# Experts ranked on the chip: 64 places for four of them, some float32 down products, and weights laid out in 4 KB rows

## The chip, the cores and the metric

One Trainium2 chip; the program runs on one of its cores. The metric is the device time of one execution in microseconds, the median over runs: lower is better.

## What is computed

A decoder trunk of two layers on 256 tokens of width 1024. Each layer has a mixing part (dilated attention beside a gated delta rule) and a channel part. The channel part of layer 1 is a choice of experts, and the change is there:

```python
logits = (x @ router_w).astype(jnp.float32)
top_val, top_idx = lax.top_k(logits, TOP_K)            # TOP_K = 2 of N_EXPERTS = 8
top_w = jax.nn.softmax(top_val, axis=-1)
gates = jnp.sum(jax.nn.one_hot(top_idx, N_EXPERTS) * top_w[..., None], axis=-2)
for e in range(N_EXPERTS):
    y = y + gates[..., e:e + 1] * swiglu(x, w_gate[e], w_up[e], w_down[e])
```

with `swiglu(x, g, u, d) = (silu(x @ g) * (x @ u)) @ d`, `g` and `u` of 1024 x 3584 and `d` of 3584 x 1024, all float32. One expert's weights are 44 MB, those of the eight 352 MB.

## The kernel before

Products need about float32 accuracy. A weight is therefore split into two float32r parts, `whi` (a cast on ACT, L100 and L102) and `wlo` (the rest, a subtraction on DVE, with GpSimd taking half of every third piece, L105). Activations are split the same way, and a row block of 128 weights costs **three products** (L414 to L416): high by high, high by low, low by high.

`Stream` (L50) holds all weights in the order of their use, in *pieces* of two row blocks by 512 columns, 512 KB. `dma_to` (L72) issues a piece's load on SP, straight from the weight matrix, in rows of 2 KB; every third piece of the experts comes as two halves in the smaller buffers (`rawh`). `advance` (L86) splits pieces ahead of their use. `caps(raw, split)` bounds the pieces loaded ahead and those split ahead; the experts have (21, 5), and (18, 5) while layer 1's output projection runs. Buffers are 36 of 4 KB and 16 of 2 KB a partition.

The experts (`moe`, L1399): `route` (L1199) finds the two experts of each token and the token's place in their lists; meanwhile `dense` (L1378) computes the first 512 hidden columns of expert 0 for all tokens. Each expert has 128 places. `gather` (L1274) takes the tokens of a pair of experts by products with one-hot rows (`Pt`). Then the experts come in order 0 to 7, each in seven chunks `c` of 512 hidden columns: `expert` (L1372) makes gate (`mg`) and up (`mu`) products, 8 row blocks each; `hidden` (L1311) makes silu(gate) times up, `hidden_t` transposes and splits it; `down` (L1359) multiplies the chunk before by its 4 row blocks of down weights for both halves `f` of the output (`oe`). `scatter` (L1342) adds an expert's result to its tokens' rows. A chunk is so 12 pieces, 24 row blocks, 72 products. Work of the helpers is put between the products by `tick`; the framework's scheduler then sets the order on each engine.

`overflow` (L1441) is a loop over all experts behind a branch, for lists longer than 128 tokens. Then comes the last normalization, and the result is written.

```python
self.CAP_MOE0 = (18, 5)
self.CAP_MOE = (21, 5)
```

Of the kernel before, what the change touches and what calls it, by code (L numbers as in the profile page):

```python
# [18 lines left out]
P = 128  # L19
# [8 lines left out]
D_EXP = 3584  # L28
NEG = -1.0e30
# [14 lines left out]

class Stream:
    """Weights in the order of their use, in pieces of two row blocks: DRAM to SBUF, then their float32 values
    split exactly into two float32r parts. caps() bounds the pieces loaded ahead and those split ahead."""

    def __init__(self, k, raw, spl):
        self.k, self.raw_cap, self.spl_cap = k, raw, spl  # L50
        self.subs = []
        self.key = {}
        self.raw = {}
        self.split = {}
        self.n_dma = 0
        self.n_split = 0
        self.retired = 0
        self.done_subs = set()
        self.share = False
        self.moe = 0  # L60
        self.SHARE, self.HALVES = 3, 3
# [4 lines left out]
    def add(self, key, src, kb, n):  # L66
        first = len(self.subs)
        for h in range(0, kb, 2):
            self.subs.append((src[:, h:h + 2], n))
        self.key[key] = list(range(first, len(self.subs)))  # L70

    def dma_to(self, i):  # L72
        while self.n_dma <= min(i, len(self.subs) - 1):
            src, n = self.subs[self.n_dma]
            q = self.k.nc.sync
            if self.n_dma >= self.moe and self.n_dma % self.HALVES == 0:
                t = [self.k.k2([P, 512], name="rawh") for _ in range(2)]
                for k in range(2):
                    q.dma_start(t[k][:, :n], src[:, k])
            else:  # L80
                t = self.k.k4([P, 2, 512], name="raw")
                q.dma_start(t[:, :, :n], src)
# [3 lines left out]
    def advance(self, need=0):  # L86
        k, nc = self.k, self.k.nc
        top = min(max(self.retired + self.spl_cap - 1, need), len(self.subs) - 1)
        while self.n_split <= top:
            i = self.n_split  # L90
            n = self.subs[i][1]
# [5 lines left out]
            if isinstance(raw, list):  # L97
                parts = [(raw[j][:, None], j, j + 1) for j in range(2)]
                for r, a, b in parts:
                    k.last_act = nc.scalar.copy(hi[:, a:b, :n], r[:, :, :n])  # L100
            else:
                k.last_act = nc.scalar.copy(hi[:, :, :n], raw[:, :, :n])  # L102
                parts = [(raw[:, j:j + 1], j, j + 1) for j in range(2)] if share else [(raw, 0, 2)]
            for r, a, b in parts:
# [21 lines left out]
class Kern:  # L126
# [7 lines left out]
    # ---------------------------------------------------------------- interleaving  # L134
# [46 lines left out]
    # ---------------------------------------------------------------- small helpers  # L181
# [36 lines left out]
    # ---------------------------------------------------------------- constants  # L218
# [47 lines left out]
        # rows of an odd block of 16 and columns of the block before it  # L266
# [18 lines left out]
    def rope_tables(self):  # L285
        """cos and sin of position * frequency, with the angle reduced exactly by multiples of 2 pi."""
# [25 lines left out]
        # [c | c] and [-s | s]  # L312
# [33 lines left out]
    # ---------------------------------------------------------------- weight plan  # L346
    def plan(self):
        W, A = self.W, self.A

        def sq(w, r0, kb, c0, n):  # L350
            return w[r0 * P:(r0 + kb) * P, c0:c0 + n].rearrange("(k p) n -> p k n", p=P)

        for l in range(DEPTH):
            wi = A["w_in"][l]
            for kg in range(2):
                W.add(("at", l, 0, 0, kg), sq(wi, 4 * kg, 4, 0, 512), 4, 512)
            for half in range(2):
                for part in range(3):
                    for kg in range(2):
                        W.add(("qb", l, half, part, kg), sq(wi, 4 * kg, 4, C_QB + part * 1024 + half * 512, 512), 4, 512)  # L360
            for g in range(3):
                for part in range(1 if g == 0 else 0, 3):
                    for kg in range(2):
                        W.add(("at", l, g, part, kg), sq(wi, 4 * kg, 4, part * 1536 + g * 512, 512), 4, 512)
                for nm, c0 in ((("z", C_Z),), (), (("ga", C_GA), ("gb", C_GB)))[g]:
                    for f in range(2):
                        for kg in range(2):
                            W.add((nm, l, f, kg), sq(wi, 4 * kg, 4, c0 + f * 512, 512), 4, 512)
            for f in range(2):
                W.add(("ba", l, f, 0), sq(A["w_branch_a"][l], 0, 4, f * 512, 512), 4, 512)  # L370
                for kg in range(2):
                    W.add(("bb", l, f, kg), sq(A["w_branch_b"][l], 4 * kg, 4, f * 512, 512), 4, 512)
            for kg in range(2):
# [1214 lines left out]
```

## Time and profile before

| | |
|---|---|
| median of three runs | 2021.1 us (2020.6 to 2021.52) |
| the profiled execution: its span | 2023.3 us; nothing further is recorded around it |
| busy in the span | PE 97%, PE's weight loads 81%, DVE 81%, ACT 63%, GpSimd 30% |
| moved | 513.65 MB, 254 GB/s mean; 278544 packets |
| weight loads' queue (SP) | 276144 packets, 504.11 MB, 70.6% of the 16 DMA engines |

Busy shares are means over stages that have different limits; slices and stretches tell them apart. Matmuls overlap in the pipeline, so PE's pace is read from the starts of neighbours and not from the duration of one (some 0.39 us). A wait is put down to the instruction that came last.

### The profile page before, as it was taken

The page shows a single profiled execution, that of the slowest core. Times are in us where ns is not written, and L with a number is a line of the kernel's source. Part 1 is how long each engine was busy: PE and PEld are TensorE (multiplying, and loading weights), DVE is VectorE, ACT ScalarE, POOL GpSimd, SP SyncE. Part 2 cuts the span into 40 slices and gives each one's busy share as a digit, 9 for nine tenths or more (in the row PEclk, how much of TensorE's full clock was granted, in tenths as well). Part 3 has the DMA queues.
Part 4 walks back from the last instruction along what each step waited for, and adds up shares of the span by engine and source line. Part 5 has one row for each costly group of instructions (what it writes and reads, how often), then busy time and mean ns, then how long its engine had stood idle before and what let it go on. Part 6 is the DMA issues. An engine that isn't in the chain of part 4 may idle for free. (4 is left out here: it accounts for less than half of the span.)

```text
span 2023.3 us, 30086 instructions
## 1 busy us (share of the span) xinstructions
PE 1960.1 (97%) x10143; PEld 1640.3 (81%) x10143; DVE 1644.2 (81%) x2208; ACT 1270.8 (63%) x1958; POOL 613.9 (30%) x484
## 2 busy tenths in 40 slices
PE   8889999999999999999999999999999999999995
PEld 7878888888888878888788788887888878888784
DVE  7886757665566976666789989999899998999997
ACT  5554546444444555554388778777787777877784
POOL 4341211000003422210334334343343433434342
PEclk9899999999999999999999999999999999999998
DMA  8344344664664353537589999999999999999991
GB/s 297 105 157 150 132 132 154 197 222 131 236 215 127 118 177 95 181 127 239 205 292 373 354 350 347 363 366 350 350 357 359 366 355 334 371 358 370 351 351 42
DMA packets 278544, 513.65 MB, mean 254 GB/s; under 512 B 29904, under 2 KB 32176, under 8 KB 278384
## 3 DMA queue, kind: packets, MB, share of 16 engines
q1 hardware_dynamic: 276144, 504.11, 70.6%
q0 software_dynamic: 2240, 7.56, 1.1%
q8 instruction: 81, 1.33, 0.3%
q14 instruction: 79, 0.65, 0.1%
HBM read 506.09 MB, written 5.51 MB: 253 GB/s over the span
## 5 line engine op out<-in xcount | busy, mean ns | idle before, releaser
L105 DVE TENSOR_TENSOR wlo<-raw,whi 128x1024 fp32r<-128x1024 f32 (+1 forms) x726 | 921.7, 1291 | 121.4 <-ACT whi L102 118.5
L102 ACT CAST whi<-raw 128x1024 fp32r<-128x1024 f32 (+1 forms) x726 | 744.8, 1046 | 78.0 <-DVE wlo L105 18.9
L105 POOL TENSOR_TENSOR wlo<-rawh,whi 128x512 fp32r<-128x512 f32 x224 | 390.7, 1744 | 593.4 <-ACT whi L100 415.3
L105 DVE TENSOR_TENSOR wlo<-rawh,whi 128x512 fp32r<-128x512 f32 x224 | 269.1, 1201 | 6.3 <-ACT whi L100 6.3
L100 ACT CAST whi<-rawh 128x512 fp32r<-128x512 f32 x448 | 256.1, 622 | 18.8 <-PE mg L415 9.8
L415 PE MATMUL oe<-wlo,hte 128*128 128x512 f32 x448 | 180.7, 403 | 0.4
L415 PE MATMUL mu<-wlo,xe 128*128 128x512 f32 x440 | 172.6, 392 | 6.6 <-DVE wlo L105 6.3
L414 PE MATMUL oe<-whi,hte 128*128 128x512 f32 x448 | 175.7, 392 | 0.0
L416 PE MATMUL oe<-whi,hte 128*128 128x512 f32 x448 | 175.2, 391 | 0.0
L414 PE MATMUL mu<-whi,xe 128*128 128x512 f32 x440 | 171.6, 390 | 0.0
L416 PE MATMUL mu<-whi,xe 128*128 128x512 f32 x440 | 171.5, 390 | 0.0
L414 PE MATMUL mg<-whi,xe 128*128 128x512 f32 x440 | 171.4, 390 | 0.0
L416 PE MATMUL mg<-whi,xe 128*128 128x512 f32 x440 | 171.4, 390 | 0.0
L415 PE MATMUL mg<-wlo,xe 128*128 128x512 f32 x440 | 171.3, 389 | 0.0
L105 POOL TENSOR_TENSOR wlo<-raw,whi 128x512 fp32r<-128x512 f32 x53 | 84.3, 1603 | 102.5 <-ACT whi L102 84.0
L566 PE MATMUL qb<-xhl,whi 128*128 128x256 f32 x384 | 113.4, 296 | 0.0
L569 PE MATMUL qb<-xhl,whi 128*128 128x256 f32 x384 | 110.9, 289 | 0.0
L571 PE MATMUL qb<-xhl,wlo 128*128 128x256 f32 x384 | 110.8, 289 | 0.0
L414 PE MATMUL at<-whi,xhl 128*128 128x512 f32 x256 | 108.1, 422 | 0.0
L415 PE MATMUL at<-wlo,xhl 128*128 128x512 f32 x256 | 102.6, 401 | 3.3 <-DVE wlo L105 3.3
L415 PEld LDWEIGHTS mu<-wlo,xe 128*128 128x128 f32 x440 | 82.6, 188 | 28.4 <-DVE wlo L105 10.9
L416 PE MATMUL at<-whi,xhl 128*128 128x512 f32 x256 | 101.9, 398 | 0.0
(421 smaller groups left out, 3875.7 us busy)
## 6 DMA issues: line engine op xcount, KB each, us to landing
raw<-in_w_in SPq DMA_DIRECT2D x168, 512.0 KB
raw<-in_moe_w_gate SPq DMA_DIRECT2D x168, 512.0 KB
raw<-in_moe_w_up SPq DMA_DIRECT2D x167, 512.0 KB
raw<-in_moe_w_down SPq DMA_DIRECT2D x113, 512.0 KB
rawh<-in_moe_w_down SPq DMA_DIRECT2D x222, 256.0 KB
rawh<-in_moe_w_up SPq DMA_DIRECT2D x114, 256.0 KB
rawh<-in_moe_w_gate SPq DMA_DIRECT2D x112, 256.0 KB
raw<-in_ffn_w_down SPq DMA_DIRECT2D x22, 512.0 KB
```

The lines of the kernel that those rows point to most:

```text
L100: k.last_act = nc.scalar.copy(hi[:, a:b, :n], r[:, :, :n])
L102: k.last_act = nc.scalar.copy(hi[:, :, :n], raw[:, :, :n])
L105: ins = (nc.gpsimd if share and a else nc.vector).tensor_tensor(lo[:, a:b, :n], r[:, :, :n], f32(hi)[:, a:b, :n], op=OP.subtract)
L414: nc.tensor.matmul(o, lhsT=xh, rhs=hi[:, kk, :n], start=st, stop=False)
L415: nc.tensor.matmul(o, lhsT=xh, rhs=lo[:, kk, :n], start=False, stop=False)
L416: nc.tensor.matmul(o, lhsT=xl, rhs=hi[:, kk, :n], start=False, stop=en)
L566: nc.tensor.matmul(o, lhsT=hi[:, kk, w], rhs=self.xhl[k // 2][:, k % 2, :S], start=(k == 0 and b % 2 == 0), stop=False, skip_group_check=True)
L569: nc.tensor.matmul(o, lhsT=hi[:, kk, w], rhs=self.xhl[k // 2][:, k % 2, S:], start=False, stop=False, skip_group_check=True)
L571: nc.tensor.matmul(o, lhsT=lo[:, kk, w], rhs=self.xhl[k // 2][:, k % 2, :S], start=False, stop=(k == 7), skip_group_check=True)
```

## The change

Weights are put in another order before the launch: every piece is one run in memory, 128 rows of 4 KB (`trunk` for everything but the experts, `moe` for those, indexed by expert and piece). `rawh` and GpSimd's part in the experts' splits go; the limits of pieces loaded ahead become 12 and 14.

On the chip `route` counts each expert's tokens and ranks the experts. Expert 0 keeps rank 0, because its first columns are under way; ranks 1 to 7 go to the others by rising count. Ranks 1 to 4 are *narrow*: 64 places. Their 64 columns of high parts and 64 of low parts of the activations stand side by side as one 128-column operand, so a row block takes **two products** (`packed`); rows 64 to 127 of the result are then folded onto rows 0 to 63 (a copy on ACT and an addition on DVE, for gate and for up). The other ranks stay at 128 places. The order of ranks is 0, 1, 5, 2, 6, 3, 7, 4: wide and narrow in turn. Which weights are loaded is known on the chip only: SP reads the expert's number into a register and adds it to the address.

Down products come one expert later, with the same chunk of the next expert; those of the last one come at the end, half by half. In wide experts the down products of chunks 0, 2, 4 and 6 use the weights and activations unsplit, as **one float32 product** (`unsplit`). The loop for overflow runs if any list is longer than its places.

```diff
+RANKS = (0, 1, 5, 2, 6, 3, 7, 4)
+NARROW = (1, 2, 3, 4)
+def moe_pieces(nm, c, j):
+    first = 12 * c + {"mg": 0, "mu": 4, "md": 8}[nm] + 2 * j
+    return first, first + 1
 class Stream:
     def dma_to(self, i):
         while self.n_dma <= min(i, len(self.subs) - 1):
-            src, n = self.subs[self.n_dma]
-            q = self.k.nc.sync
-            if self.n_dma >= self.moe and self.n_dma % self.HALVES == 0:
-                t = [self.k.k2([P, 512], name="rawh") for _ in range(2)]
-                for k in range(2):
-                    q.dma_start(t[k][:, :n], src[:, k])
-            else:
-                t = self.k.k4([P, 2, 512], name="raw")
-                q.dma_start(t[:, :, :n], src)
+            src, n, _ = self.subs[self.n_dma]
+            if callable(src):
+                src = src()
+            t = self.k.k4([P, 2, 512], name="raw")
+            self.k.nc.sync.dma_start(t[:, :, :n], src[:, :2 * n].rearrange("p (k n) -> p k n", k=2))
...
     def advance(self, need=0):
...
+            if plain:
+                self.split[i] = (raw, None, 2, n)
+                self.n_split += 1
+                self.dma_to(self.n_split + self.raw_cap - 1)
+                continue
...
-            share = self.share or (i >= self.moe and i % self.SHARE == 0)
+            share = self.share
...
     def plan(self):
...
+            def src():
+                if r not in self.reg:
+                    self.reg[r] = self.nc.values_load(self.eidi[0:1, r:r + 1], engines=(mybir.EngineType.SP,), min_val=0,
+                                                      max_val=NE - 1)
+                return A["moe"][bass.ds(self.reg[r], 1), j].rearrange("o p n -> (o p) n")
...
+        for i, r in enumerate(RANKS):
+            for c in range(7):
+                for nm in ("mg", "mu"):
+                    for kg in range(2):
+                        add(nm, r, c, kg)
+                if i:
+                    for f in range(2):
+                        add("md", RANKS[i - 1], c, f)
+        for f in range(2):
+            for c in range(7):
+                add("md", RANKS[-1], c, f)
+    def plain(self, r, c):
+        return r not in NARROW and c in self.PLAIN
...
     def route(self):
...
+        cnt = self.small([P, 3, 8], "cnt")
+        nc.vector.tensor_copy(cnt[:, 0], ps[:, 0:8])
+        nc.vector.scalar_tensor_tensor(cnt[:, 1], cnt[:, 0], 8.0, io8, op0=OP.mult, op1=OP.add)
+        nc.vector.memset(cnt[:, 1, 0:1], -1.0)
...
+        nc.vector.tensor_tensor(m8[:, 0], col(cnt[:, 1]), row(cnt[:, 1]), op=OP.is_lt)
+        nc.vector.tensor_reduce(cnt[:, 2], m8[:, 0], axis=AX.X, op=OP.add)
...
     def hidden(self, res, key):
...
+        def folded(a, dst):
+            if not nar:
+                return a
+            nc.scalar.copy(dst[:64], a[64:])
+            nc.vector.tensor_tensor(dst[:64], dst[:64], a[:64], op=OP.add)
+            return dst[:64]
...
+    def packed(self, keys, o, x, first=True, last=True):
...
+                nc.tensor.matmul(o, lhsT=x(k0 + kk), rhs=hi[:, kk], start=first and i == 0 and kk == 0, stop=False)
+                nc.tensor.matmul(o, lhsT=x(k0 + kk), rhs=lo[:, kk], start=False, stop=last and end)
...
+    def unsplit(self, keys, o, x, first=True, last=True):
...
+                nc.tensor.matmul(o, lhsT=x(k0 + kk), rhs=w[:, kk], start=first and i == 0 and kk == 0, stop=last and end)
...
     def moe(self):
...
+                if i:
+                    self.run(self.down(RANKS[i - 1], c))
+        for f in range(2):
+            for c in range(7):
+                self.run(self.down(RANKS[-1], c, (f,)))
...
     def overflow(self):
...
-        with tc.If(n > P):
+        with tc.If(n > 0):
...
     def build(self):
...
-        self.CAP_MOE0 = (18, 5)
-        self.CAP_MOE = (21, 5)
+        self.CAP_MOE0 = (12, 5)
+        self.CAP_MOE = (14, 5)
+        self.PLAIN = (0, 2, 4, 6)
```

The order on PE, before, where an expert's down products end and the gate products of the next chunk begin (`hte` is the transposed hidden part, `xe` the gathered tokens):

```order
L414 MATMUL oe<-whi,hte 128x512
L415 MATMUL oe<-wlo,hte 128x512
L416 MATMUL oe<-whi,hte 128x512
L414 MATMUL mg<-whi,xe 128x512
L415 MATMUL mg<-wlo,xe 128x512
L416 MATMUL mg<-whi,xe 128x512
L414 MATMUL mg<-whi,xe 128x512
```

Now, in the first narrow expert (`xen`; lines are those of the changed kernel). `htp` is the unsplit hidden part, `raw` the weights as they were loaded:

```order
L1495 MATMUL mg<-wlo,xen 128x512
L1494 MATMUL mg<-whi,xen 128x512
L1439 MATMUL ht<-ident,mgs 128x128 x4
L1508 MATMUL oe<-raw,htp 128x512
L1495 MATMUL mg<-wlo,xen 128x512
L1494 MATMUL mg<-whi,xen 128x512
L1495 MATMUL mg<-wlo,xen 128x512
L1494 MATMUL mg<-whi,xen 128x512
```

Three products a row block have become two, and the down products, with one float32 product each, stand between gate products. The weights of this first `oe` are the ninth piece of the chunk, while those of the gate products around it are the first and second.

The order on DVE, before, at the end of a chunk:

```order
L105 TENSOR_TENSOR wlo<-rawh,whi 128x512
L105 TENSOR_TENSOR wlo<-raw,whi 128x1024
L1322 TENSOR_TENSOR mgs<-mgs,mu 128x512
L105 TENSOR_TENSOR wlo<-raw,whi 128x1024
L105 TENSOR_TENSOR wlo<-rawh,whi 128x512
L105 TENSOR_TENSOR wlo<-raw,whi 128x1024 x2
L1339 TENSOR_TENSOR hte<-ht,hte 128x4x128
```

Now, for one chunk of a narrow expert whose down part is float32:

```order
L162 TENSOR_TENSOR wlo<-raw,whi 128x1024 x7
L1414 TENSOR_TENSOR mgs<-mgs,mg 64x512
L162 TENSOR_TENSOR wlo<-raw,whi 128x1024 x2
L1414 TENSOR_TENSOR mus<-mus,mu 64x512
L1425 TENSOR_TENSOR mgs<-mgs,mus 64x512
L1447 TENSOR_TENSOR htn<-ht,htn 128x4x64
L162 TENSOR_TENSOR wlo<-raw,whi 128x1024 x5
```

The halves `rawh` are gone, so every split is 1024 columns on DVE; the folds (L1414) and the narrower second part (`htn`) have come in.

The order on SP now, where the last of the experts' numbers are read (`eidi`; the loads ahead are those of expert 0, whose address is fixed; `cnti` tells whether the overflow loop runs):

```order
L418 TENSOR_LOAD eidi
L418 ISA x2
L418 TENSOR_LOAD eidi
L418 ISA x2
L140 DMA raw<-in_moe 128x1024 x2
L1591 TENSOR_LOAD cnti
L1591 ISA x2
L140 DMA raw<-in_moe 128x1024 x2
L140 ISA
L140 DMA raw<-in_moe 128x1024
L140 ISA
```

Before, SP had loads alone here, with fixed addresses. Now it reads seven numbers between the 33rd and the 53rd piece of the experts, and behind the loads of rank 0 each load has a register operation (`ISA`) of its own.

## Rows read from the trace of the kernel before

**Rows 1.** The page's second part: busy tenths of PE, DVE and the DMA engines, and GB/s, in 40 slices of 50.6 us.

```profile
PE   8889999999999999999999999999999999999995
DVE  7886757665566976666789989999899998999997
...
DMA  8344344664664353537589999999999999999991
GB/s 297 105 157 150 132 132 154 197 222 131 236 215 127 118 177 95 181 127 239 205 292 373 354 350 347 363 366 350 350 357 359 366 355 334 371 358 370 351 351 42
```

**Rows 2.** Busy time of each engine by stretches of the second half: stretch, length, then busy us (instructions) of PE, PEld (weight load), DVE, ACT and POOL, granted clock, DMA share, GB/s.

```profile
993.00:1030.00 37.00, 36.51 (x204) 29.94 (x203) 28.49 (x66) 21.03 (x36) 10.14 (x8) 1.00 0.48 164
...
1196.00:1316.00 120.00, 119.66 (x554) 98.42 (x553) 113.27 (x106) 94.37 (x132) 46.66 (x28) 1.00 0.96 346
...
1556.00:1676.00 120.00, 118.50 (x537) 97.19 (x536) 114.23 (x102) 91.65 (x126) 48.43 (x28) 1.00 1.00 366
1676.00:1796.00 120.00, 119.66 (x553) 98.42 (x552) 113.14 (x105) 93.94 (x133) 46.70 (x27) 1.00 0.96 345
```

**Rows 3.** Waits between 1200 and 1900 us: engine, line, what it waited for: us in total, times, longest.

```profile
PEld mu L415 <- DVE wlo L105: 7.2, 8, 1.8
...
PE mu L415 <- DVE wlo L105: 3.5, 5, 1.4
```

**Rows 4.** The same stretch, waits of SP's DMA queue (L79 and L82 issue the weight loads).

```profile
SPq L79 <- DVE wlo L105: 203.9, 110, 5.7
SPq L79 <- PE oe L415: 54.9, 30, 1.9
```

**Rows 5.** PE's instructions in order of time, the first and the last of 42 products: start us, duration us, engine, line, out<-in.

```profile
1502.28 0.39 PE L414 MATMUL mg<-whi,xe 128*128 128x512 f32 x1
...
1511.57 0.39 PE L416 MATMUL mu<-whi,xe 128*128 128x512 f32 x1
```

**Rows 6.** PE's instructions on the tile `mg` over the whole run: count, durations in ns, first and last start.

```profile
L414 PE MATMUL mg<-whi,xe x440: 387/389/479, 1024.0 to 1982.1; 128*128 128x512 f32 x147
```

**Rows 7.** PE in order of time, the last product of the experts.

```profile
2002.11 0.40 PE L416 MATMUL oe<-whi,hte 128*128 128x512 f32 x1
```

**Rows 8.** The page's fifth part: one of the three products of a row block, for each kind of weights (count | busy us, mean ns | idle before).

```profile
L415 PE MATMUL oe<-wlo,hte 128*128 128x512 f32 x448 | 180.7, 403 | 0.4
L415 PE MATMUL mu<-wlo,xe 128*128 128x512 f32 x440 | 172.6, 392 | 6.6 <-DVE wlo L105 6.3
...
L415 PE MATMUL mg<-wlo,xe 128*128 128x512 f32 x440 | 171.3, 389 | 0.0
```

**Rows 9.** PE in order of time at the float32 products of `kkq` (x8 is eight records, two for a product); `qb` are split products of 256 columns.

```profile
98.36 0.28 PE L569 MATMUL qb<-xhl,whi 128*128 128x256 f32 x1
98.48 0.28 PE L571 MATMUL qb<-xhl,wlo 128*128 128x256 f32 x1
98.61 1.89 PE L728 MATMUL kkq<-kq 128*128 128x256 f32 x8
100.15 0.47 PE L566 MATMUL qb<-xhl,whi 128*128 128x256 f32 x1
100.45 0.28 PE L569 MATMUL qb<-xhl,whi 128*128 128x256 f32 x1
```

**Rows 10.** Groups of instructions between 1200 and 1900 us: line, engine, operation, out<-in, shape, count | busy us, mean ns | idle time before and what ended it.

```profile
L105 DVE TENSOR_TENSOR wlo<-raw,whi 128x1024 fp32r<-128x1024 f32 x315 | 423.7, 1369 | 13.2 <-ACT whi L102 13.0
L102 ACT CAST whi<-raw 128x1024 fp32r<-128x1024 f32 x316 | 327.5, 1051 | 23.2 <-PE mg L415 10.0 <-PE oe L416 5.9 <-issue 2.8
L105 POOL TENSOR_TENSOR wlo<-rawh,whi 128x512 fp32r<-128x512 f32 x159 | 276.7, 1740 | 426.4 <-ACT whi L100 299.4 <-DVE wlo L105 36.7 <-DMA raw<-in_moe_w_gate 24.5
...
L1322 DVE TENSOR_TENSOR mgs<-mgs,mu 128x512 f32<-128x512 f32 x39 | 26.7, 684 | 10.3 <-ACT whi L100 7.5 <-issue 1.6 <-PE mu L416 1.2
...
L1356 DVE TENSOR_TENSOR x<-x,sc 128x512 f32<-128x512 f32 x24 | 15.4, 685 | 7.0 <-PE sc L1354 7.0
...
L1349 DVE SCALAR_TENSOR_TENSOR ol<-oe,gs,oh 128x512 fp32r<-128x512 f32 x12 | 8.9, 744 | 0.1
...
L1307 DVE COPY gs<-PT 128x1 f32<-128x1 f32 x6 | 0.9, 152 | 0.9 <-ACT PT L1306 0.9
```

**Rows 11.** DVE in order of time in a stretch of the trunk where GpSimd shares no split.

```profile
405.94 2.36 DVE L105 TENSOR_TENSOR wlo<-raw,whi 128x1024 fp32r<-128x1024 f32 x2
408.21 0.75 DVE L213 TENSOR_TENSOR xhl<-tp,xhl 128x256 fp32r<-128x256 f32 x2
```

**Rows 12.** A number read from SBUF into SP's registers and the register operation behind it (L1444): durations min/median/max in ns.

```profile
L1444 SPq TENSOR_LOAD <-cnti x1: 463/463/463, 1021.8 to 1021.8; - x1
L1444 SPq FUSED_REGOPS  x1: 181/181/181, 1022.3 to 1022.3; - x1
```

**Rows 13.** Issues of loads into the tile `raw`: durations min/median/max in ns, first and last start.

```profile
L82 SPq DMA_DIRECT2D raw<-in_moe_w_gate x168: 367/406/1343, 959.3 to 1946.1; - x168
```

**Rows 14.** Stretches as in rows 2: one in which only the copies of zeros of L282 move, and two in the experts.

```profile
42.00:44.00 2.00, 2.00 (x19) 2.00 (x18) 2.00 (x7) 1.79 (x3) 1.20 (x1) 1.00 0.91 369
1240.00:1242.00 2.00, 2.00 (x11) 1.65 (x10) 2.00 (x3) 1.74 (x3) 1.08 (x1) 1.00 1.06 409
1260.00:1280.00 20.00, 20.00 (x91) 16.48 (x90) 19.11 (x19) 16.16 (x23) 7.64 (x6) 1.00 1.03 390
```

More of the change, by code (lines that the diff above doesn't have):

```diff
@@ new lines, in plan, with piece @@
+        first = 0
+        for key, _, _, _, kb, _, n in trunk_blocks():
+            W.add(key, [A["trunk"][first + j] for j in range(kb // 2)], n)
+            first += kb // 2
+        self.reg = {}
+        def piece(r, j):
+            if r == 0:
+                return A["moe"][0, j]
+            def src():
[3 more added lines that the diff above has]
+                return A["moe"][bass.ds(self.reg[r], 1), j].rearrange("o p n -> (o p) n")
+            return src
@@ new lines, in route @@
+        eid = self.small([P, 8], "eid")
+        by_rank(eid, io8)
+        self.eidi = self.small([P, 8], "eidi", 1, I32)
+        nc.vector.tensor_copy(self.eidi, eid)
+        yield
+        self.rk0, self.gt0 = rk, gt
+        self.rk = self.small([P, 2, 8], "rkr")
+        self.gt = self.small([P, 2, 8], "gtr")
+        for t in range(2):
+            by_rank(self.rk[:, t], rk[:, t])
+            by_rank(self.gt[:, t], gt[:, t])
+        yield
+        cap = self.small([P, 8], "cap")
+        nc.vector.memset(cap, float(P))
@@ L1262, in route, with place @@
+        self.cnti = self.small([P, 1], "cnti", 1, I32)
+        nc.vector.tensor_copy(self.cnti, cnt[:, 1, 0:1])
         for t in range(2):
             nc.scalar.mul(self.x[t], self.x[t], ALPHA)
[L1265 removed]
+    def place(self, i):
         nc = self.nc
[L1268 to L1269 removed]
+        self.Pt[i] = Pt = self.k2([P, 2, 2, P], F32R, name="Pt")
+        for r in RANKS[max(2 * i - 1, 0):2 * i + 1]:
             for t in range(2):
[L1271 to L1272 removed]
@@ L1357, in scatter, with down @@
             yield
-    def down(self, e, c):
+    def down(self, r, c, fs=(0, 1)):
         if c == 0:
-            self.oe = [self.bg("oe"), self.bg("oe")]
-        self.finish([("ht", e, c)])
-        ht = self.ht.pop((e, c))
-        def xf(k, t):
-            return ht[:, k - 4 * c, :P], ht[:, k - 4 * c, P:]
-        for f in range(2):
-            yield from self.gemm([(("md", e, c, f), 4 * c)], {0: self.oe[f]}, xf, first=(c == 0), last=(c == 6), tiles=(0,))
-            if c == 6:
-                self.add_chain(self.scatter(e, f, self.oe[f]), ("scat", e, f), 1)
@@ L1372, in expert @@
-    def expert(self, e, c, nm):
-        a = self.acc(nm)
-        xf = hlf(self.xe[e // 2])
-        yield from self.gemm([((nm, e, c, kg), 4 * kg) for kg in range(2)], {e % 2: a}, xf, tiles=(e % 2,))
+            if fs[0] == 0:
+                self.oe = {}
+            for f in fs:
+                self.oe[f] = self.bg("oe")
+        self.finish([("ht", r, c)])
+        ht = self.ht[r, c]
+        for f in fs:
+            keys, ends = [(("md", r, c, f), 0)], dict(first=(c == 0), last=(c == 6))
+            if r in NARROW:
+                yield from self.packed(keys, self.oe[f], lambda k: ht[:, k], **ends)
+            elif self.plain(r, c):
+                yield from self.unsplit(keys, self.oe[f], lambda k: ht[:, k], **ends)
+            else:
+                yield from self.gemm(keys, {0: self.oe[f]}, lambda k, t: (ht[:, k, :P], ht[:, k, P:]), tiles=(0,), **ends)
+            if c == 6:
+                self.add_chain(self.scatter(r, f, self.oe[f]), ("scat", r, f), 1)
@@ L1376, in expert @@
+    def expert(self, r, c, nm):
+        a = self.acc(nm)
+        keys = [((nm, r, c, kg), 4 * kg) for kg in range(2)]
+        x = self.xe[r]
+        if r in NARROW:
+            yield from self.packed(keys, a, lambda k: x[:, k])
+        else:
+            yield from self.gemm(keys, {0: a}, lambda k, t: (x[k // 4][:, k % 4, :P], x[k // 4][:, k % 4, P:]), tiles=(0,))
         return a
```

289 lines of the change are left out of this document (162 added, 127 removed).

## The prediction

> **What bounds the kernel now.** I read the page's forty slices first. They show two halves: up to slice 20 TensorE (PE) is 8 to 9 tenths busy mostly at 100 to 240 GB/s, behind it PE, VectorE (DVE) and the DMA engines all stand at 9 tenths and some 350 GB/s [rows 1]. The change works almost wholly in the second half, the experts. Their busy time by stretches of 120 us says the same in numbers: of each 120 us PE is busy 118.5 to 119.7, DVE 113 to 114, ScalarE (ACT) 92 to 94, and the DMA share is 0.96 to 1.00 at 345 to 366 GB/s [rows 2]. Three resources look full, so the waits have to say which one ends last. PE's longest waits for a split weight part amount to 3.5 us and 7.2 us in 700 us [rows 3], while SyncE (SP), which issues the weight loads, stands 203.9 us waiting for DVE to give back a buffer and 54.9 us for PE [rows 4]. So loads wait for room, and room for products: **PE is the bound**. A busy PE need not be PE at its peak, so I take its pace from starts: 42 products follow each other from 1502.28 to 1511.57, which is 9.29 / 41 = 0.2266 us for one of 512 columns [rows 5]. The experts proper begin with the first `mg<-whi,xe` at 1024.0 [rows 6] and their last `oe` product starts at 2002.1 [rows 7]: 978 us. That holds 3 × (448 + 440 + 440) = 3984 products [rows 8]; at the pace, and a granted clock of 1.00 [rows 2] (the 2.4 GHz level), they fill 902.8. The other 75.5 us are transposes, gathers, scatters and small waits: **1.37 us for each of 55 chunks**. Behind the last product lie 21.2 us to the span's end at 2023.3, which the change leaves alone.
>
> The profiled execution is 2.2 us above the median of the three runs (2021.1). I sum against its span and subtract 2.2 at the end.
>
> **The change, part by part.** *Two products for three.* The four narrow experts have 4 × 7 × 24 row blocks of 128 weights; each saves one product: 672 × 0.2266 = 152 us of PE. *Float32 down products.* Four wide experts take chunks 0, 2, 4, 6 of their down matrix unsplit: 128 products in place of 384. The price is that of a float32 product. The nearest row is the 128x256 one of `kkq`, two records for a product: eight records and one split product of 256 columns take 98.61 to 100.45, the latter 0.12, so a record takes 0.215 and a product 0.43, or 0.86 for 512 columns [rows 9]. From below it can't cost less than one split product (0.23); from above, if the eight records overlapped with nothing, 1.89 / 4 = 0.47, or 0.94 for 512. I take 0.86, since columns scale. That is 8 × 0.86 − 24 × 0.2266 = 1.4 us more in each of 16 chunks, 23 us in all. It spares ACT and DVE 64 of 672 splits.
>
> *PE's new sum, by stages.* The order is now wide, narrow, wide, and so on, with the down products of the expert before. A chunk costs: first expert 48 × 0.2266 + 1.37 = 12.2 (6 of them); narrow expert 32 × 0.2266 + 8 × 0.86 + 1.37 = 15.5 where the down part is float32 (4 of 7), 56 × 0.2266 + 1.37 = 14.1 where not (3 of 7); wide expert 64 × 0.2266 + 1.37 = 15.9 (7). At the end 28 pieces of down products of a narrow expert: 112 × 0.2266 + 2.6 = 28. Together 73 + 4 × 104.3 + 3 × 111.1 + 28 = 852 us, against 978.
>
> *DVE.* It loses GpSimd's help with the splits (159 halves in 700 us) [rows 10], but a split that shares nothing with GpSimd is shorter: two take 405.94 to 408.21, 1.135 each [rows 11], against a mean of 1.369 [rows 10]. Each narrow chunk adds two folds and a smaller second half; a 512-column operation is 0.68 [rows 10], and I give 64 rows the same (no less than half of it, no more than the whole). A narrow stage then needs 68 × 1.135 + 21 × 0.68 + 7 × 0.35 + 4 × 0.685 + 2 × 0.744 for the scatter [rows 10] = 98 us, a wide one 84 × 1.135 + 12 = 107: both under PE's 104 and 111. ACT's casts at 1.05 [rows 10] and its two folds a chunk come to less. These parts I cost at nothing, under PE; without that cover a narrow chunk with split downs is DVE's at 12 × 1.135 + 3.1 = 16.7 us.
>
> *The ranking* adds some 20 small operations on DVE behind one count and delays the first lists; a one-column copy takes 0.15 us [rows 10], so they make 3 us, with their waits up to 6, once. I put all 6 on the path: the experts proper start at 1030. *SP* now reads seven numbers (0.46 us each) and does a register operation (0.18) for each of some 600 loads [rows 12]; a load's issue has a median of 0.41 [rows 13], so 0.6 us for each piece of 1.3: under cover. Trunk loads with 4 KB rows lie under a PE at 8 to 9 tenths while the DMA engines are at 3 to 6 [rows 1]; nothing. The lower limits of loads ahead (12 and 14 for 18 and 21) delay the first weights of the experts; from 993 to 1030 the DMA share is 0.48 [rows 2], which makes that good.
>
> *The loads.* They become the thing that is late next. A piece is 524 KB and a chunk with down products 6.29 MB; PE's 15.5 us would ask 406 GB/s. What 4 KB rows give is not shown for weights, so I bound it. From below: no gain, 366 GB/s [rows 2]. From above: in 42 to 44 us only the zero copies, whose packets are 4 KB, move, 369 GB/s at a share of 0.91, or 405 at a full share [rows 14]; 2 KB rows in their best 2 us give 409 at 1.06, or 386 [rows 14]. With the share that the experts hold, about 0.98, I take 405 × 0.98 = 397 GB/s, and 425 (405 × 1.05) as the end. At the end of the first expert, 1030 + 73 = 1103.5, the limits 14 and 5 let 19 pieces lie ahead, so 672 − 75 = 597 are to come, 313 MB: 788 us at 397. The last weight lands at 1892, its split and products end at 1896. PE alone would end at 1030 + 852 = 1882. The two are so near that they cost each other something: in the order, float32 down products stand ahead of gate products whose weights land earlier, so PE waits for a piece eight places on. I put 10 us on that. **Sum:** 1906 + 21.2 = 1927, less 2.2: **1925 us**.
>
> The Trainium skill (DMA: Bandwidth & Descriptors, Why small descriptors are slow) gives a packet a fixed cost of about three beats of 32 B, so going from 2 to 4 KB would gain 67/64 over 131/128, 2.3%. By that figure the rate would be 386 × 1.023 × 0.98 = 387 and the sum, an estimate, 1945; the rows here give 405 over 386, 4.9%, if from another kind of copy.
>
> **The rivals.** *A: the loads keep up.* At 425 GB/s they take 736 us and PE alone ends the stage, at 1882: 1882 + 21 − 2 = **1901**. For it: 409 GB/s appears in a short stretch already [rows 14]. Against it: the share never stays above 1.00 over 120 us [rows 2].
> *B: longer rows give nothing.* At 366 GB/s the 313 MB take 855 us: 1103.5 + 855 + 14 + 19 = **1991**. For it: the share is 1.00 at 366 [rows 2]. Against: 390 GB/s over 20 us with 2 KB rows [rows 14], so 366 is what PE asked for and no ceiling.
> The Trainium skill (HBM Reference, Specifications) puts a core's part of the memory at about 358 GB/s; by that the change would end near 2011, an estimate, and the trace, with 409, does not agree while the other core is idle.
> *C, slower: the lists overflow.* If the fourth smallest of experts 1 to 7 has more than 64 tokens, the rest goes through the loop at the end, which takes every expert's 168 row blocks, 1344 float32 products of 0.86 in a row, for 128 more places each: 1156 us at least, so **3081**. The reference's own draw gives lists of 80, 75, 60, 46, 63, 64, 52, 72 tokens: the four smallest are 46, 52, 60, 63 and fit with one to spare; three of eleven other draws that I counted would not.
> *D: it gains nothing on the whole*, since splits, folds and loads at 95% each stall one another: the 126 us that PE saves come back as waits, each chunk at its old 17.8 us: about **2020**. Against it: SP's long waits show buffers full, so today's near-full engines hardly stall PE [rows 3, 4].
>
> **How the numbers follow.** My forecast 0.62, A 0.14, B 0.13, C 0.05, D 0.06. The range runs from 1893, just below A, to 1990, the end of B. About 0.2% (4 us) is what a measurement can tell from no change; faster by more: forecast, A, B and a part of D, 0.91; within it 0.02; slower 0.07.
>
> **What would show it.** Right: a start-to-start pace of 0.227 in `packed`, 0.86 a product in `unsplit`; weights at 385 to 410 GB/s at a share near 1 from 1100 to 1880; DVE splits at 1.14 with GpSimd idle; PE busy less than before and waiting for raw pieces. Wrong: a rate under 375 GB/s at a full share (B); PE without waits (A); work behind the branch of the overflow (C); DVE waiting for folds (D).

## The result and the profile after

| | before | changed |
|---|---|---|
| median of the runs | 2021.1 us | 2049.3 us (2048.7 to 2052.1) |
| ratio to before | | 1.0143, 95% interval 1.0129 to 1.0158 |
| span of the profiled execution | 2023.3 us | 2047.0 us |

The change is slower by 1.4%; 1925 was predicted. The slices of the changed kernel's page (tenths busy, and GB/s) answer to [rows 1]. The first half is as it was. Behind slice 20 PE is below its 9 in places, and the loads move no more than before.

```profile
PE   8989999999999999999999889998899988999886
DVE  7885747655568966666787769887788877888778
DMA  8344435654753343536589999999999999999993
GB/s 293 104 174 139 136 125 166 216 196 135 248 203 115 144 148 121 161 112 229 201 295 361 322 359 342 351 356 339 356 332 351 359 330 353 338 358 372 332 343 119
```

The first `mg<-whi,xe` starts at 1023.0 (1024.0 before), so ranking and trunk cost nothing, and 20 us lie behind the last `oe` product (21 before): **all of the loss lies in the experts**, 1004 us from first to last product for 978 [rows 6, 7]. The windows by stage (a narrow, a wide, a narrow, a wide expert; columns: us, then busy time and count of PE, PEld, DVE, ACT, POOL, granted clock, DMA share, GB/s) answer to [rows 2]:

```profile
1098.00:1229.80 131.80, 114.47 (x404) 74.31 (x404) 97.70 (x101) 80.55 (x99) 0.00 (x0) 0.95 0.95 348
1229.80:1351.00 121.20, 118.48 (x514) 89.29 (x513) 106.35 (x104) 92.34 (x116) 0.00 (x0) 1.00 0.95 347
1351.00:1483.00 132.00, 114.53 (x412) 73.52 (x410) 100.72 (x106) 82.13 (x101) 0.00 (x0) 0.97 0.95 350
1483.00:1605.00 122.00, 119.26 (x514) 90.19 (x513) 105.92 (x103) 92.30 (x116) 0.00 (x0) 0.99 0.93 343
```

A narrow expert takes 132 us for a predicted 104, a wide one 121 for 111. No engine is full in a narrow one: PE is busy 114 to 115 us, DVE 98 to 101, ACT 81 to 82 of 132, and the granted clock is below 1.00. The waits from 1100 to 1800 (engine, tile and line, whom it waits for, us, times, longest), which answer to [rows 3], tell of engines that wait in a ring. ACT's copies that fold the halves and its activation wait for PE, DVE's adds and splits for ACT, PE's products for both:

```profile
ACT mgs L1413 <- PE mg L1495: 59.2, 19, 3.9
ACT mus L1413 <- PE mu L1495: 54.8, 19, 4.1
DVE wlo L162 <- ACT whi L160: 44.2, 86, 2.5
DVE mus L1414 <- ACT mus L1413: 41.9, 21, 3.5
ACT mgs L1419 <- PE mg L456: 39.6, 16, 4.3
...
PEld oe L1495 <- DVE wlo L162: 21.1, 47, 0.7
```

One chunk's end in a narrow expert shows how (timeline: start, us, engine, line, operation, and in brackets the idle time before it and its releaser):

```profile
1656.21 1.02 PE L1508 MATMUL oe<-raw,htp 128*128 128x512 f32 x2
...
1656.41 0.58 ACT L1413 COPY mus<-mu 64x512 f32<-64x512 f32 x1 [4.15 <-PE mu L1495]
1657.02 0.68 DVE L1414 TENSOR_TENSOR mus<-mus,mu 64x512 f32<-64x512 f32 x1 [3.50 <-ACT mus L1413]
1657.74 0.68 DVE L1425 TENSOR_TENSOR mgs<-mgs,mus 64x512 f32<-64x512 f32 x1
...
1658.57 0.43 PE L1439 MATMUL ht<-ident,mgs 64*128 64x64 f32 x4 [1.34 <-DVE mgs L1425]
1659.03 0.37 ACT L1446 CAST htn<-ht 128x256 fp32r<-128x256 f32 x1 [2.04 <-PE ht L1439]
1659.30 4.83 ACT L160 CAST whi<-raw 128x1024 fp32r<-128x1024 f32 x5
...
1660.40 0.79 PE L1494 MATMUL mg<-whi,xen 128*128 128x512 f32 x1 [1.41 <-ACT whi L160]
...
1661.66 0.79 PE L1495 MATMUL mg<-wlo,xen 128*128 128x512 f32 x1 [0.47 <-DVE wlo L162]
...
1662.25 0.63 PE L1494 MATMUL mg<-whi,xen 128*128 128x512 f32 x1
...
1662.68 0.63 PE L1495 MATMUL mg<-wlo,xen 128*128 128x512 f32 x1
```

The last `mu` product is out at 1656.2, and behind it PE has one float32 down product left (two records); the other seven of the chunk had been put ahead, among gate, up and earlier down products. So it stands while copy, add, product and transposes go round ACT and DVE. The casts of the next gate pieces stand behind `htn` in ACT's queue and begin at 1659.30, though their raw pieces landed long ago (from landing to cast start a piece lies 18 us, the median from 1100 to 1800, worked out from landing times and cast starts). Products then follow each other at 0.43 us and no longer at 0.23. The windows before, in and behind the gap show the granted clock at 1.00, 0.95 and 0.58: behind some 4 us with four short transposes alone, PE runs for a while at its lower level, 1.2 GHz.

```profile
1640.00:1656.00 16.00, 16.00 (x59) 10.68 (x58) 11.46 (x12) 8.44 (x10) 0.00 (x0) 1.00 0.92 345
1656.00:1660.40 4.40, 1.66 (x8) 0.68 (x6) 1.80 (x4) 1.95 (x4) 0.00 (x0) 0.95 1.02 412
1660.40:1668.00 7.60, 7.13 (x18) 5.33 (x19) 5.75 (x5) 3.96 (x5) 0.00 (x0) 0.58 0.80 287
```

Over the stage 1351 to 1484, PE's starts come to 22.9 us of standing and 7.3 us of slower products more than the pace of 0.227: 30 us, where the stage missed the prediction by 28 (the small work was a little less). The lower clock is the small part of it: 18 products of the stage follow each other at 0.43 us, some 4 us, and the stage's mean clock is 0.97. The larger part is standing, at the transposes and behind them for splits and casts.

### The profile page after: what moved, and what is told of

Read it like the earlier page. It is cut to its first block, busy times and chain, and to the rows that moved or that the text cites. A ratio compares the mean times of both kernels' runs of the same rounds, so it can differ in the third digit from the quotient of the medians.

```text
span 2047.0 us, 28316 instructions
## 1 busy us (share of the span) xinstructions
PE 1914.3 (94%) x9375; PEld 1493.1 (73%) x9375; DVE 1536.1 (75%) x2207; ACT 1201.6 (59%) x1758; POOL 227.0 (11%) x264
## 5 line engine op out<-in xcount | busy, mean ns | idle before, releaser
L162 DVE TENSOR_TENSOR wlo<-raw,whi 128x1024 fp32r<-128x1024 f32 (+1 forms) x886 | 1027.8, 1199 | 167.6 <-ACT whi L160 163.2
L160 ACT CAST whi<-raw 128x1024 fp32r<-128x1024 f32 x886 | 880.0, 1046 | 58.3 <-DVE wlo L162 20.2
L1508 PE MATMUL oe<-raw,htp 128*128 128x512 f32 x256 | 129.1, 593 | 0.0
L1495 PE MATMUL mu<-wlo,xen 128*128 128x512 f32 x224 | 116.1, 518 | 12.3 <-DVE wlo L162 12.3
L1495 PE MATMUL mg<-wlo,xen 128*128 128x512 f32 x224 | 109.8, 490 | 7.5 <-DVE wlo L162 7.5
L1494 PE MATMUL mg<-whi,xen 128*128 128x512 f32 x224 | 100.0, 447 | 11.3 <-ACT whi L160 11.3
L1495 PE MATMUL oe<-wlo,htn 128*128 128x512 f32 x224 | 96.6, 431 | 8.3 <-DVE wlo L162 8.3
L1494 PE MATMUL mu<-whi,xen 128*128 128x512 f32 x224 | 90.5, 404 | 8.4 <-ACT whi L160 8.4
L454 PE MATMUL mg<-whi,xe 128*128 128x512 f32 x216 | 85.7, 397 | 0.0
L456 PE MATMUL mg<-whi,xe 128*128 128x512 f32 x216 | 84.8, 392 | 0.0
L454 PE MATMUL mu<-whi,xe 128*128 128x512 f32 x216 | 84.5, 391 | 0.0
```

Source lines behind the costliest of these rows:

```text
L162: ins = (nc.gpsimd if share and a else nc.vector).tensor_tensor(lo[:, a:b, :n], r[:, :, :n], f32(hi)[:, a:b, :n], op=OP.subtract)
L454: nc.tensor.matmul(o, lhsT=xh, rhs=hi[:, kk, :n], start=st, stop=False)
L456: nc.tensor.matmul(o, lhsT=xl, rhs=hi[:, kk, :n], start=False, stop=en)
L1494: nc.tensor.matmul(o, lhsT=x(k0 + kk), rhs=hi[:, kk], start=first and i == 0 and kk == 0, stop=False)
L1495: nc.tensor.matmul(o, lhsT=x(k0 + kk), rhs=lo[:, kk], start=False, stop=last and end)
L1508: nc.tensor.matmul(o, lhsT=x(k0 + kk), rhs=w[:, kk], start=first and i == 0 and kk == 0, stop=last and end)
```

## The experiments

Four theories were open: **VectorE** (splits without GpSimd), **fold** (its copies and adds), **loads** (rate or buffers) and, from the ninth run on, **order** (the issue order that the scheduler writes for PE, ACT and DVE). The last column has the second narrow expert and the wide one behind it, each from its first `mg` product to the next expert's first.

| run | median us | ratio to before, 95% interval | narrow, wide stage us |
|---|---|---|---|
| changed kernel | 2049.3 | 1.0143 (1.0129 to 1.0158) | 132.6, 122.0 |
| e1 rows of 2 KB | 2049.4 | 1.0133 (1.0116 to 1.0150) | 134.1, 122.2 |
| e2 no fold | 2009.8 | 0.9950 (0.9933 to 0.9967) | 124.0, 121.6 |
| e3 half the subtract | 1999.2 | 0.9882 (0.9866 to 0.9899) | 124.8, 119.6 |
| e4 half the loads | 1920.3 | 0.9504 (0.9486 to 0.9522) | 105.7, 114.2 |
| e5 light, 4 KB | 1897.5 | 0.9388 (0.9373 to 0.9404) | |
| e6 light, 2 KB | 1938.2 | 0.9590 (0.9574 to 0.9606) | |
| e7 half the bytes | 1929.2 | 0.9549 (0.9533 to 0.9565) | 106.8, 115.9 |
| e8 one slot, two pieces more | 2053.7 | 1.0167 (1.0150 to 1.0184) | 133.1, 121.2 |
| e9 down products last | 2033.4 | 1.0062 (1.0044 to 1.0080) | 128.7, 121.6 |
| e12 and longer lead | 2031.0 | 1.0059 (1.0042 to 1.0076) | 128.7, 121.6 |
| e13 no float32 | 2048.8 | 1.0137 (1.0120 to 1.0154) | 132.9, 120.5 |
| e14 e9 and GpSimd | 2109.4 | 1.0453 (1.0430 to 1.0476) | 140.7, 130.2 |
| **f1 order of e7, all bytes** | **1938.2** | **0.9588 (0.9559 to 0.9617)** | 107.1, 118.4 |
| f2 half the bytes, old order | 2049.9 | 1.0149 (1.0130 to 1.0168) | 132.7, 122.2 |
| g2 new order on ACT, DVE alone | 2099.4 | 1.0393 (1.0376 to 1.0410) | 140.0, 129.7 |
| g3 new order on PE alone | 2024.6 | 1.0022 (1.0013 to 1.0032) | 119.2, 129.0 |
| h1 f1 with rows of 2 KB | 1964.1 | 0.9726 (0.9710 to 0.9743) | 113.1, 118.5 |
| i1 no float32, its own good order | 1980.9 | 0.9808 (0.9785 to 0.9831) | 118.0, 116.4 |

**Taking work away: e1 to e4.**

```diff
 e1  lay_out: - reshape(2, P, n).swapaxes(-3, -2)     + reshape(2, P, n)
 e2  folded:  - copy a[64:], add a[:64]               + return a[:64]
 e3  advance: - lo[:, 0:2] = raw - hi                 + lo[:, 0:1] = raw - hi   (PE reads it for both)
 e4  dma_to:  + for every second piece: t = self.last (no load)
```

> The changed kernel with every weight piece stored as two blocks of 128 rows of 2 KB instead of 128 rows of 4 KB; nothing else differs. Theory VectorE (splits at 1.20 us a piece without GpSimd's help set the pace) and theory fold (the copies and adds that fold the halves make the in-order queues wait): 2049 within 6 us. Theory loads, if longer rows cost rate: each of eight stages 4 to 5% shorter, about 2005. If longer rows give rate, as predicted (397 against 366 GB/s), and loads bind: longer, 2080 or more.

> Leaves out the fold in the four experts with 64 places: only rows 0 to 63 of the gate and up sums are read, so 56 ACT copies and 56 DVE adds are gone and the low part of the tokens is left out of the result. Theory fold: the four narrow stages fall from 132 us to about 105, so 1945 (1935 to 1960). Theory VectorE: only the adds' own time goes, 14 x 0.68 = 9.5 us a narrow stage, so about 2010. Theory loads: stages can't fall below 44 MB at 372 GB/s = 118 us, so about 1995.

> Leaves out half of VectorE's split in the experts: only the low part of a piece's first row block is computed and used for both, so a split takes DVE about 0.6 us instead of 1.20; ACT, PE and the loads do the same work. Theory VectorE: wide stages 121 to 111 us and narrow ones 132 to about 110, 2049 - 4 x 10 - 4 x 20 = about 1925. Theory fold: the waits for PE stay, about 2035. Theory loads: no stage under 118 us, about 1990.

> Leaves out half of the experts' loads: every second piece uses the tile that the piece before it loaded, so the loads ask for half the bytes and half the raw buffers; casts, splits and products are as many as before. Theory loads (rate or buffers): wide stages to 111, narrow ones to 105 or little more, about 1930. Theories VectorE and fold: 2049 within 10 us.

Longer rows change nothing here. Without the fold 40 us come back, as theory VectorE had it; with half the subtract 50, where VectorE asked for 125 and loads for 60; with half the loads 129, as theory loads had it. No theory fits all four; loads fits best, and that reading was to turn out wrong.

**What the loads can do: e5 to e8.**

```diff
 e5  advance: + experts: hi = copy(raw); no lo          gemm, packed: - product with lo
 e6  e5 with e1's layout
 e7  dma_to:  - dma_start(t, src[:, :2 * n])  + dma_start(t[:, 0], src[:, :n]); t[:, 0:1] read for both
 e8  - n4, n2 = 36, 16; CAP_MOE = (14, 5)     + n4, n2 = 37, 14; CAP_MOE = (16, 5)
```

> Leaves out the low parts of the experts' weights (no second part, no product with it; from the second chunk of the first expert on), so that VectorE has no splits and TensorE one product where it had two, two where it had three; all loads and casts stay. Nothing but the loads can then set the pace: it measures what they give with 4 KB rows. From 1023 us 338 MB are to come: 397 GB/s, as predicted, would end at about 1905; 375 GB/s at 1955; 366 at 1975. If the theory is that buffers, not the rate, bind, the DMA share falls under 0.9 only where consumers are slow, which here they aren't: 397 and 1905.

> The same light kernel with rows of 2 KB: what longer rows are worth when nothing else binds. Prediction's premise (rows of 4 KB gain 3 to 5% of rate): 20 to 45 us slower than the light kernel with 4 KB rows. No gain from rows: the same within 8 us.

> Leaves out half of every expert piece's bytes: a load brings the first row block (128 rows of 2 KB), both halves are read from it; as many loads, raw tiles and buffers as in the changed kernel, and the same casts, splits and products. Theory rate (the DMA engines' bytes per us bind): about 1925, as with half the loads. Theory buffers (loads are issued too late, because raw tiles come free too late): little gained, 2010 to 2040.

> One more 4 KB slot (37 for 36, two fewer of 2 KB) and 16 pieces loaded ahead in place of 14. Theory buffers: bursts of demand are bridged by a longer lead, each stage 2 to 4 us shorter, about 2025. Theory rate alone: 2049 within 5 us.

The same windows of the light kernel with 4 KB and with 2 KB rows (columns as above):

```profile
1100.00:1800.00 700.00, 574.22 (x1972) 344.54 (x1973) 106.65 (x178) 552.02 (x685) 0.00 (x0) 0.89 1.02 404
```

```profile
1100.00:1800.00 700.00, 559.06 (x1896) 333.48 (x1894) 101.68 (x170) 529.80 (x657) 0.00 (x0) 0.88 1.04 384
```

So loads give 404 GB/s with 4 KB rows and 384 with 2 KB, and neither is what the changed kernel moved (347). There SP waited for buffers; in the light kernel for earlier loads (first SP wait of each from 1100 to 1800):

```profile
SPq L140 <- DVE wlo L162: 145.2, 127, 6.4
```

```profile
SPq L140 <- DMA raw<-in_moe: 303.4, 417, 1.5
```

Loads issued and not yet landed are 3.7 on average in the changed kernel and 7.2 in the light one (worked out from issue and landing times). The low rate then looks like a result: loads follow consumers who are late (f1 below shows it). But e7, with the same count of loads and buffers, again gained all, and more room (e8) nothing. The way out of the contradiction was in the order: with half the bytes the scheduler had written another one (as it reckons with the time of loads; that this is the reason was not tested by itself). In e4 and e7 four or more of a chunk's eight float32 products stand behind its last `mu` product, in the changed kernel one, but for the first chunk of a stage.

**The order on PE by a rule: e9, e12, e13, e14.**

```diff
 e9   unsplit: + with self.behind(self.up):          (self.up: the chunk's last up product)
                     nc.tensor.matmul(o, ...)
 e12  e9, and advance: the limit of 5 counts split pieces only
 e13  - PLAIN = (0, 2, 4, 6)                          + PLAIN = ()
 e14  e9, and share = self.share or (expert piece and i % 3 == 0)
```

> The changed kernel with one rule of issue order more: a float32 down product stands on PE behind the last up product of its chunk, as the program writes it, and no longer among the gate and up products, where the scheduler had put 8 of the 16 records or more. Products, splits, loads and buffers are the same. Theory order (the moved down products leave PE nothing to do while the fold, activation and transposes run, it stands some 4 us a chunk and then runs at the 1.2 GHz level): the four narrow stages fall from 132 to about 110 us, so about 1960. Theory loads in flight (few pieces outstanding, 335 GB/s at 3 to 5 of them): no stage below 118, 1995 to 2010. Theory VectorE: its 100 us of work a narrow stage is queued as before, 2035 or more.

> The same rule, and the limit of five pieces split ahead counts only pieces that are split, not the float32 ones, so that up to four more may be split while the down part runs. Theory order: 5 to 15 us less than with the rule alone, since the next gate products find their parts ready. Theory loads in flight: no less, or up to 10 us more, since split parts take buffers from loads.

> The changed kernel without float32 products: all down pieces are split and take three products in the wide experts (PLAIN empty). PE's sum for a narrow stage falls by 1.4 us x 4 to 99, DVE's rises by 16 splits to 120. Theory order: nothing is moved ahead, the narrow stages follow VectorE, 118 to 122, so 1995 to 2010. Theory VectorE (1.20 us a split is the pace): 125 or more a narrow stage, 2020 or more. If float32 products cost nothing but their time: 2043.

> The rule of the first of these and GpSimd doing half of every third split in the experts, as in the kernel before. Theory VectorE: 17 us less work on it in a wide stage, 6 to 8 us less in each stage than with the rule alone, so 40 us less. Theory order or loads: within 10 us of the rule alone, or slower, since GpSimd's half takes 1.6 us and lengthens others.

The rule gives 16 us of the 90 that theory order promised, and the lead adds nothing clear (2 us). Without float32 products the kernel stays at 2049, where theory order had 1995 to 2010. So the moved float32 products are not the cause by themselves, and theory order, as an order on PE alone, missed twice, while theory VectorE, with 2035 and 2020 or more, was near. In e9 all eight float32 products stand behind the last `mu`, and PE no longer waits for `mgs` before the transposes (16.7 us from 1100 to 1800 in the changed kernel). But ACT still stands before `htn`, with the casts behind it, and PE's wait for splits at `mu` has grown from 9.2 us to 21.8 (e9's waits, 1100 to 1800):

```profile
ACT htn L1446 <- PE ht L1439: 29.9, 14, 2.8
...
PE mu L1495 <- DVE wlo L162: 21.8, 42, 0.8
```

GpSimd's help costs 76 us. e14's splits from 1100 to 1800 by form (count, busy us, mean ns, idle before):

```profile
L162 DVE TENSOR_TENSOR wlo<-raw,whi 128x1024 fp32r<-128x1024 f32 x270 | 360.5, 1370 | 38.8 <-ACT whi L160 38.2 <-DMA raw<-in_moe 0.4 <-PE oe L1495 0.3
L162 POOL TENSOR_TENSOR wlo<-raw,whi 128x512 fp32r<-128x512 f32 x123 | 218.6, 1778 | 483.2 <-ACT whi L160 447.5 <-PE oe L1494 16.7 <-PE mg L455 6.9
L162 DVE TENSOR_TENSOR wlo<-raw,whi 128x512 fp32r<-128x512 f32 x123 | 142.2, 1156 | 8.3 <-ACT whi L160 8.0
```

A half split beside GpSimd keeps DVE 1.156 us, a whole one in the changed kernel 1.218: the help saves next to nothing, and e14's whole splits take 1.370. So e14 gave DVE no less work, and it is no test of theory VectorE.

**Bytes and order crossed: f1, f2.** Both orders were written down and imposed on the other kernel as edges of order alone, from the experts on:

```diff
+ for engine in (PE, Activation, DVE):
+     q = [instructions of the engine in the order of the table]
+     for a, b in zip(q, q[1:]):
+         self.tc.add_manual_dep(b, a.name, NoSync)
```

> The changed kernel, all its loads and work, with the issue order of PE, ACT and DVE from the experts on taken from the kernel that loads half the bytes (a table of numbers, edges of order only). That kernel differed from the changed one in two things: the bytes, and the order that the scheduler made, since it reckons with the loads' time. Theory order (the queues' order is what costs): about 1930 to 1950, as with half the bytes, or 1950 to 1970 where loads then bind. Theory bytes: 2030 to 2049, as in the changed kernel.

> The other half of the cross: half of every expert piece's bytes, as before, but PE, ACT and DVE in the issue order of the changed kernel. Theory order: 2030 to 2045, little gained though half the bytes move. Theory bytes: 1929 within 10 us.

This decides it: with all bytes and the other order 1938, with half the bytes and the old order 2050. **The order costs 111 us, the bytes 9** (with the old order, nothing). f1 is faster than both kernels. It also settles the other theories: all splits are still on DVE at 1.218 us each, all folds and all loads are there, and a narrow stage takes 107 us. The same place in f1 (timeline):

```profile
1367.96 2.74 PE L1520 MATMUL oe<-raw,htp 128*128 128x512 f32 x6
1368.16 0.58 ACT L1425 COPY mus<-mu 64x512 f32<-64x512 f32 x1 [2.92 <-PE mu L1507]
...
1368.65 1.99 ACT L172 CAST whi<-raw 128x1024 fp32r<-128x1024 f32 x2
1368.78 0.68 DVE L1426 TENSOR_TENSOR mus<-mus,mu 64x512 f32<-64x512 f32 x1 [3.07 <-ACT mus L1425]
...
1370.63 0.46 PE L1451 MATMUL ht<-ident,mgs 64*128 64x64 f32 x4
1371.02 1.13 PE L1520 MATMUL oe<-raw,htp 128*128 128x512 f32 x2
1371.12 0.37 ACT L1458 CAST htn<-ht 128x256 fp32r<-128x256 f32 x1 [0.49 <-PE ht L1451]
...
1371.58 0.79 PE L1506 MATMUL mg<-whi,xen 128*128 128x512 f32 x1
```

Six records, three products, run while the chain goes round, one more behind the transposes, and ACT casts two pieces between `mus` and `htn`. The next gate products find their parts split; none of these rows of PE has a wait. The windows of f1 and f2:

```profile
1100.00:1800.00 700.00, 682.05 (x2881) 509.20 (x2881) 638.18 (x646) 545.28 (x666) 0.00 (x0) 1.00 1.01 394
```

```profile
1100.00:1800.00 700.00, 641.48 (x2480) 445.19 (x2478) 562.91 (x566) 470.91 (x579) 0.00 (x0) 0.97 0.54 173
```

In f1 the clock is 1.00 and the loads move 394 GB/s; in f2 PE waits as before with DMA half idle.

**Which engine's order, and the terms under a good one: g2, g3, h1, i1.** g2 and g3 impose a part of f1's tables (g2: ACT and DVE, with PE's old one; g3: PE alone, with ACT and DVE left to the scheduler), h1 is f1 with e1's layout, i1 is e13 with the order of its own half-byte twin.

> The changed kernel, all loads, with ACT and DVE in the order of the half-byte kernel and PE in the order that it has in the changed kernel (both written down as order edges). If PE's order (float32 down products moved forward) is the cause: 2020 to 2045. If the order of casts, splits, folds and activations on ACT and DVE is: 1940 to 1965. If they must fit each other: between, 1980 to 2010.

> The counterpart: PE alone in the order of the half-byte kernel, ACT and DVE as the scheduler then puts them, which is nearer to the changed kernel's order than to the half-byte kernel's. If PE's order is the cause: 1940 to 1965. If ACT's and DVE's is: 2025 to 2045, as with the rule that put the down products last (2033).

> The kernel with the half-byte kernel's order on all three engines (1938 us) and rows of 2 KB in place of 4 KB. There the DMA share is 1.00 at 388 GB/s with 5.6 loads in flight, so rows should now matter: by the light kernels (403 and 383 GB/s) eight stages at 110 to 115 us in place of 108 to 112, so 1955 to 1965. If rows matter only where nothing else works: 1938 within 6.

> No float32 down products (all pieces split), with the order taken in the same way from its own half-byte twin: what the float32 part is worth once order doesn't cost. By the prediction's terms it costs PE 23 us and spares DVE 64 splits. If PE bounds: 1915 to 1925. If DVE does (84 splits of 1.21 and 17 us of folds a narrow stage, 122 us): 1975 to 2000.

Neither engine's order is the cause alone: PE's gives 25 us, ACT's and DVE's make it 50 us worse, both together give 111. They must fit each other. g2's longest wait of PE is now for the product of the hidden parts (g2's waits, 1100 to 1800):

```profile
PE ht L1451 <- DVE mgs L1437: 76.3, 36, 4.2
```

Under the good order the two terms that showed nothing before are there: 4 KB rows are worth 26 us (1964 to 1938), the float32 products 43 (1981 to 1938, each kernel under an order of its own); without them DVE is at 0.95:

```profile
1100.00:1800.00 700.00, 664.73 (x2846) 496.49 (x2845) 668.38 (x674) 567.91 (x684) 0.00 (x0) 0.99 0.98 376
```

e13 and i1 do the same work in two orders, and there too the order costs 68 us (2049 and 1981), with no float32 product at all. The traces show what the two good orders have in common in most chunks of a narrow stage. On ACT, five casts stand between the copy `mus` and the cast `htn` of a chunk with split down products (two in the changed kernel, e9 and e13), and two in a float32 chunk of f1 (none in the changed kernel and e9). On PE, 23 or 24 of a split chunk's 24 down products stand between the last `mu` and the transposes (seven in the others). So in f1 and i1 both engines have work while the ring goes round.

What stays open: which pair of places in the tables carries how much of the 111 us (the common places above were read from the traces and not tested singly), and how low an order made for these durations could go.

## Why the prediction was wrong

- **PE's sum by stages: near as a sum of work.** With a fitting order the stages take 74 us (73 predicted), 105 to 107 (104.3) and 117 to 118 (111.1; the 6 are small waits). A float32 product costs the 0.86 us taken from [rows 9]: its two records start 0.43 us apart, the next product starts 0.03 later, and that one holds up its follower by 0.41.
- **The loads: right as a rate, wrong as what comes late.** 397 GB/s was predicted; f1 moves 394 and the light kernel 404. Rows of 4 KB gain 5% in the light kernels, as 405 over 386 in [rows 14] had it. The Trainium skill (DMA: Bandwidth & Descriptors, Why small descriptors are slow) led to an estimate of 2.3%; the runs show more. The 358 GB/s that the prediction took from the Trainium skill (HBM Reference, Specifications) is, by the same section, a core's share when both cores of a pair stream; a core alone is said to measure well above it, and the 404 here agree. The prediction set its trace against that page without need. Rival B is refuted as a ceiling, though the changed kernel's 347 GB/s looks like it and longer rows gave it nothing (e1).
- **The failed step is the cover: "These parts I cost at nothing, under PE", and "I put 10 us on" the order.** DVE's sum for a narrow stage was near (98 against 98 to 101 measured, though a split takes 1.218 and not 1.135), but a sum under PE's is cover only if the queues let the work run beside it. That float32 down products stand ahead of gate products was seen, and priced as a wait for a load. What it costs is that little work is left on PE behind the last up product while copy, add, product, transposes and cast go round. That is a part only: with the down products put back (e9) 16 us come back, with PE's whole new order (g3) 25. The other 86 come when ACT's and DVE's orders fit it too (g3 to f1): in the changed kernel casts and splits stand behind instructions that wait for PE, and the prediction has no term for that. Together the orders cost 111 us where it had 10. With f1's order the time is 1938, 13 us above the forecast, and in part by luck: with half the bytes as well (e7) it is 1929, where PE's sum alone gave 1901 (rival A's number), and all the bytes cost 9 us, where the forecast has 24 for the loads and their wait.
- **Rival D** (2020, 0.06) was nearest: engines that stall one another. Its reason was another, engines at 95% each; in a narrow stage DVE is at 0.74 to 0.76 and ACT at 0.61 to 0.62, and they stall by their order. It also set no loss beyond the old time, and the loss is 28 us. The argument against it failed: SP's long waits [rows 4] do show full buffers, but in the changed kernel the buffers are full of pieces whose casts stand behind a waiting instruction (18 us from landing to cast), and PE waits all the same.
- **Rival C** did not occur: the lists fit, and no work runs behind the branch. **Rival A** needed 425 GB/s; no run's mean from 1100 to 1800 is above 404. The ranking's 6 us did not show: the experts start at 1023.0, not at 1030.

## What to carry to other kernels

An engine's sum of work says what it needs, the order of its queue says when: where a change shortens the bounding engine's work, walk one period of the new order by hand, from the last product of one step round the other engines to the first of the next, and price what PE has left to do meanwhile. If a scheduler writes the order, a change of sizes or bytes rewrites it on all engines; so an experiment that takes work away must hold the order fixed, or it tests two things. A part of a good order can be worse than none of it (g2: 50 us).

## What the runs showed of the hardware

- The granted clock fell to 0.58 in the window behind a gap of some 4 us in which PE did four transposes; products there took 0.43 us for 0.23. In that kernel's stage from 1351 to 1484 standing cost 22.9 us and the lower clock some 4.
- Packets of 4 KB on always busy DMA engines gave 404 GB/s, of 2 KB 384; with 3.7 loads in flight for 7.2 the same rows gave 347.
- With GpSimd doing half of every third split, DVE's own half took 1.156 us and its whole splits 1.370, for 1.218 in the kernels without it: the sharing spared DVE nothing.
